# Two-layer mLSTM and band-attention trunk on one core: attention's PSUM banks, late gate transposes, rows by GpSimd's queue, modulation sums in quarters

## The chip, the cores and the metric

The kernel runs on one core of a Trainium2 chip. The metric is device time in microseconds of one execution; the time before is the median of three runs. TensorE (PE in the profile) multiplies, VectorE (DVE) and ScalarE (ACT) work element by element, GpSimd (POOL) takes a small part, and SyncE (SP) issues DMAs. PEld is PE's loading of weights. On each engine instructions run in the order in which they stand in the program; an instruction that waits holds up those behind it.

## The reference

512 tokens, model width 2048, fp32, two layers and a key/value projection between them:

```
mod  = silu(c) @ ada_w[l] + ada_b[l]             # shift, scale, gate: 3 x 2048 per layer
h    = rmsnorm(x, g_pre) * (1 + scale) + shift
layer 0: proj = h @ w_in (2048 x 16400); q, k = silu(causal_conv(...)); v, o, z; 8 mLSTM heads
         y = sigmoid(o) * rmsnorm(heads) * silu(z);  y @ w_out (4096 x 2048)
kmod = silu(c) @ kv_ada_w + kv_ada_b             # shift and scale of the shared key/value input
k, v = (rmsnorm(x, kv_g) modulated by kmod) @ kv_w
layer 1: q, z = h @ b_w_in; 16 heads: softmax(q k / sqrt(128) + relative bias, band) v
         (o * silu(z)) @ b_w_out
x    = x + gate * rmsnorm(y, g_post)             # after each layer
```

With 512 tokens and chunks of 64 with 8 chunks to the left, the band is causal by chunks over the whole sequence.

## The kernel before

Every fp32 operand of a large product is split into a rounded part and a rest (`split`, L186: a cast on ACT, a subtraction on DVE, L189), and `mm3` (L258) makes three matmuls of them. The weights of all products lie in one stream (`wst`): SP loads a raw tile (`wr`), ACT casts it to `wh`, DVE subtracts to `wl`, and in products of the Strassen kind (`proj_s`) DVE, from the keys on POOL, forms sums `ws` (L216) that are split too. PSUM is cut into five banks for projections (`newp`) and three for everything else (`newa`).

A scheduler sets the order on each engine: it follows the program, except that work under `high_priority` (weights, evacuations) is drawn forward, and instructions under `keep_in_program_order` keep their place among each other. Work that is to run beside a projection is hung on it as a hook, a function called before the weight piece of that number (`at={k: f}`).

The stages, with the start in the profiled execution: the modulation, normalised rows and the first v products (0 to 210 us); the v rows of heads 4 to 7 (`proj_b`, 210); eight mLSTM heads (411), each two `proj_s` for q and k and four for o and z, with scores, rows of v and the normaliser between; the output product `a_w_out` in four column groups, first half of the inner width, then second half, there by pairs of row tiles (1480); then residual, turning into columns (`turned`, `ps_x`, L914), values of columns 0 and 1 (1868), keys (1968), values 2 and 3 (2155), attention heads (2250), `b_w_out` (2643).

What the change and the prediction touch:

- **The modulation sums.** A column of `mod` is a dot product of `silu(c)` with 2048 weights on 128 partitions. It is done on DVE in two halves of 1024: a load of 512 KB, a multiply-and-sum, and a read of the accumulator. `background` (L602) does 64 halves (gate of layer 0, and `HALF_KV` = 16 of the 32 columns of `kmod`) beside the v rows; `late_half` (L619) does 96 more, 72 beside `a_w_out` (`first_half`) and 24 in the keys (`kv_half`); `last_gates` (L1225) does the 32 of the last gate beside `b_w_out`, and `gates_end` turns each four columns into a row (`ps_gg`, L646).
- **The gates** of the mLSTM (`gates`, L533): a long chain of 8x512 operations on DVE and ACT that ends in four small transposes into `ps_at` (L576).
- **Head sums** (`head_sums`, `head_splits`): sums of the input rows for `proj_s`, needed by the first head.
- **Rows.** `y_tile` (L843) loads the heads' results (`yr`, two buffers, 512 KB) by SP; `residual` (L879) loads the input rows `xr` by SP just before it needs them, sums squares (`sqx`) and stores; `keyed` loads `xp` by POOL's queue.
- **Attention.** `weights` (L1115) makes four score tiles `ps_s` in four tiles of three banks, then the softmax; `flipped` (L1136) transposes the weights into `ps_t`, four tiles in three banks: the tenth transpose needs the bank of the first group again, so it stands behind that group's `split`.

## Time and profile before

| | us |
|---|---|
| median of 3 runs | 2849.38 (2848.09 to 2855.21) |
| the profiled execution's own time | 2849.11 |
| its span, first to last instruction | 2847.3 |
| PE busy | 2769.4 (97%) |
| DVE busy | 2299.7 (81%) |
| ACT busy | 1507.1 (53%) |
| POOL busy | 335.5 (12%) |
| mean granted TensorE clock | 0.993 |

In the profile a group is named by its line in the kernel before, its engine, its operation and `out<-in`; an arrow in brackets with a time is the idle time of the engine before the instruction and what ended it. "Stretch" tables give the busy time of each engine between two times. The ends of matmuls are modelled, so a busy PE may still run below its pace.

### The profile page before, as it was taken

Reading aid. Unit: us, or ns where it says so; the run is one execution under the profiler, and the core shown is the slowest. Engines: PE = TensorE matmul, PEld = TensorE weight load, DVE = VectorE, ACT = ScalarE, POOL = GpSimd, SP = SyncE. Lnnn points to the kernel's source line nnn. Section 1 sums busy time; section 2 is a strip of 40 time slices with the busy share of each in tenths; the row PEclk is TensorE's granted clock in tenths of the full one; section 3 lists DMA queues with packets and bytes.
Section 4 is the critical chain, followed back from the end, with each engine's and each line's share of the span. In section 5 each row is a group of like instructions: output and inputs, shape, how many; then the busy total and the mean of one; then the engine's idle time right before and its main releaser. Section 6 shows DMA issues by size and latency. Waiting matters only on the chain.

```text
span 2847.3 us, 45749 instructions
## 1 busy us (share of the span) xinstructions
PE 2769.4 (97%) x17066; PEld 2481.5 (87%) x17066; DVE 2299.7 (81%) x4108; ACT 1507.1 (53%) x2576; POOL 335.5 (12%) x308
## 2 busy tenths in 40 slices
PE   7999999999999999999999999999999999999998
PEld 5787878999999999999998878877888899999877
DVE  7976689898989898888886676668996888888755
ACT  4222236575757575757564232477335566666523
POOL 0000000000000000000000000001660455554000
PEclk9999999999999999999999999999999999999999
DMA  8886973332323333333337886787556533333875
GB/s 325 306 301 241 300 244 110 107 123 101 127 102 123 113 115 112 112 112 112 118 109 255 298 313 231 244 290 262 204 189 212 176 120 124 131 126 124 290 256 182
DMA packets 173145, 529.39 MB, mean 186 GB/s; under 512 B 18629, under 2 KB 27365, under 8 KB 172281
## 3 DMA queue, kind: packets, MB, share of 16 engines
q1 hardware_dynamic: 172282, 524.38, 53.5%
q8 instruction: 133, 2.18, 0.3%
q0 software_dynamic: 640, 2.10, 0.2%
q14 instruction: 90, 0.74, 0.1%
HBM read 484.40 MB, written 47.24 MB: 187 GB/s over the span
## 4 chain that ended last, share of the span: by engine, by line
PE 70%; DVE 12%; DMA 11%; issue 4%; ACT 2%; SPq 0%; DVEq 0%; ACTq 0%; POOL 0%; POOLq 0%
PE ps_y L261 9%; PE ps_azo L261 8%; PE ps_bzo L261 6%; DVE wl L189 5%; PE ps_czo L261 5%; PE ps_dzo L261 5%; DMA ada<-in_adaT 4%; PE ps_azq L261 4%; DMA al<-in_adaT 4%; PE ps_kv L261 4%; PE ps_l L261 3%; PE ps_bzq L261 3%; PE ps_cz L261 2%; PE ps_czq L261 2%; PE ps_dzq L261 2%
## 5 line engine op out<-in xcount | busy, mean ns | idle before, releaser
L188 ACT CAST wh<-wr 128x384 fp32r<-128x384 f32 (+2 forms) x816 | 550.2, 674 | 939.5 <-PE ps_y L261 226.9
L189 DVE TENSOR_TENSOR wl<-wr,wh 128x384 fp32r<-128x384 f32 (+2 forms) x816 | 643.8, 789 | 259.2 <-ACT wh L188 240.7
L261 PE MATMUL ps_y<-wh,y 128*128 128x512 f32 x1536 | 479.6, 393 | 0.0
L189 DVE TENSOR_TENSOR wl<-ws,wh 128x512 fp32r<-128x512 f32 x477 | 375.8, 788 | 0.0
L261 PEld LDWEIGHTS ps_y<-wh,y 128*128 128x128 f32 x1536 | 290.5, 189 | 60.8 <-DVE z L355 0.2
L261 PE MATMUL ps_y<-wl,y 128*128 128x512 f32 x768 | 301.4, 392 | 2.6 <-DVE wl L189 2.6
L188 ACT CAST wh<-ws 128x512 fp32r<-128x512 f32 x477 | 294.1, 617 | 9.3 <-DVE ws L216 5.1
L261 PE MATMUL ps_azo<-h,wh 128*128 128x256 f32 (+1 forms) x1024 | 232.1, 311 | 0.0
L216 POOL TENSOR_TENSOR ws<-wr 128x512 f32<-128x512 f32 (+1 forms) x96 | 138.8, 1446 | 407.6 <-DVE wl L189 243.7
L216 POOL TENSOR_TENSOR ws<-ws,wr 128x256 f32<-128x256 f32 (+1 forms) x192 | 181.5, 945 | 15.0
L261 PEld LDWEIGHTS ps_y<-wl,y 128*128 128x128 f32 x768 | 145.5, 189 | 33.8 <-DVE wl L189 3.8
L261 PEld LDWEIGHTS ps_azo<-h,wh 128*128 128x128 f32 x1024 | 166.1, 191 | 8.5
L766 POOL TENSOR_TENSOR nmd<-nm,maskd 128x512 f32<-128x512 f32 x8 | 10.5, 1317 | 1365.3 <-DVE sp_q L189 922.5
L261 PE MATMUL ps_kv<-wh,hkv 128*128 128x512 f32 x512 | 160.6, 392 | 1.1 <-DVE hkv L189 0.9
L261 PE MATMUL ps_v<-wh,h 128*128 128x512 f32 x512 | 159.8, 393 | 0.0
L261 PE MATMUL ps_azo<-h,wl 128*128 128x256 f32 (+1 forms) x512 | 158.7, 310 | 0.0
L261 PE MATMUL ps_bzo<-h,wh 128*128 128x256 f32 (+1 forms) x640 | 156.7, 326 | 0.0
L261 PE MATMUL ps_czo<-h1s,wh 128*128 128x256 f32 x768 | 146.9, 283 | 0.0
L216 DVE TENSOR_TENSOR ws<-ws,wr 128x256 f32<-128x256 f32 (+1 forms) x384 | 135.0, 353 | 3.0
L261 PE MATMUL ps_l<-wh,h 128*128 128x512 f32 x384 | 120.7, 391 | 3.1 <-ACT wh L188 3.0
L261 PEld LDWEIGHTS ps_czo<-h1s,wh 128*128 128x128 f32 x768 | 120.3, 192 | 0.7
L261 PE MATMUL ps_azq<-h,wh 128*128 128x256 f32 (+1 forms) x512 | 117.1, 313 | 1.9 <-ACT wh L188 1.9
(339 smaller groups left out, 6890.0 us busy)
## 6 DMA issues: line engine op xcount, KB each, us to landing
wr<-in_wst SPq DMA_DIRECT2D x512, 512.0 KB, 3.8
ada<-in_adaT SPq DMA_DIRECT2D x160, 512.0 KB, 6.0
al<-in_adaT SPq DMA_DIRECT2D x96, 512.0 KB, 4.8
xt<-nsc SPq DMA_DIRECT2D x48, 256.0 KB, 4.6
ysc<-zo SPq DMA_DIRECT2D x32, 256.0 KB, 2.5
yr<-ysc SPq DMA_DIRECT2D x16, 512.0 KB, 5.5
vr<-vrow SPq DMA_DIRECT2D x24, 256.0 KB, 4.3
bsc<-in_ext SPq DMA_DIRECT2D x16, 320.0 KB, 6.1
```

Source lines behind the costliest of these rows:

```text
L188: cast = nc.scalar.copy(hi, src)
L189: nc.vector.tensor_tensor(lo, src, hi.bitcast(F32), op=ALU.subtract)
L216: add = lambda o, a, b: summer[0].tensor_tensor(o, a, b, op=ALU.add)
L261: nc.tensor.matmul(ps, a, b, start=start, stop=stop)
L766: nc.gpsimd.tensor_tensor(nmd, nm.rearrange("p (a b) -> p a b", a=4), maskd.unsqueeze(1).to_broadcast([P, 4, P]), op=ALU.add)
```

## The change

Five edits:

1. Attention. Scores 0 and 2 share one bank (128 + 384 columns) and are made in the order 0, 2, 1, 3; the transposes 2 and 3 share one bank (256 + 128), and all ten are issued before the first split.
2. Small gate transposes. `gates_turned` is a hook of the next head's v rows instead of the end of `gates`; `gates_end` is replaced by `last_gates(g, 0)` and, some pieces later, `gates_out`.
3. `yr` and `xr` are loaded by GpSimd's queue.
4. `xr` has buffers of its own and is loaded ahead (`residual_rows`): row tiles 0 and 1 at the start of the last column group of pair 0, 2 and 3 within the next; a copy of one column from `ssq` holds each load back to that place.
5. Modulation. Of the 32 columns of `kmod`, 8 instead of 16 go in the background (48 halves), 16 go into the heads as 64 quarters of 512 (256 KB loads), eight per head; the remaining late halves are 80, of which eight stand beside pair 0 of `a_w_out`, and none in the keys. The hooks of `turned(1)` move by two pieces.

```
-HALF_KV = 16
+HALF_KV = 8
+QUARTERS = 16
@@ gates
         nc.sync.dma_start(gsc[1], w)
+
+    def gates_turned():
         pt = newa("ps_at")
         for j in range(4):
-            nc.tensor.transpose(pt[:, j * 8 : j * 8 + 8], e[:, j * P : (j + 1) * P], ident[:8, :8])
+            nc.tensor.transpose(pt[:, j * 8 : j * 8 + 8], ssum[:8, j * P : (j + 1) * P], ident[:8, :8])
@@ late sums
+    heads_end = 96 + HALF_KV + QUARTERS
+    late_cols = [*range(heads_end, 128)], [*range(48, 64)], [*range(64, 80)]
+    quarters = [(j, i) for j in range(4) for i in range(96 + HALF_KV, heads_end)]
+    def late_part(parts, w, sc, tile=None):
         for j, i, t in begun:
             tc.keep_in_program_order(nc.vector.tensor_tensor_reduce(
...
+        j, i = parts.pop(0)
+        if sch[0] != (j, w):
+            sch[:] = (j, w), sc([P, w], F32, tag="sc", name=f"sch{w}_{i}_{j}")
+            nc.sync.dma_start(sch[1], scd[j * w : (j + 1) * w].partition_broadcast(P))
+        t = tile([P, w], F32, tag="al", name=f"al{w}_{j}_{i}")
+        tc.keep_in_program_order(nc.sync.dma_start(t, adaT[i, :, j * w : (j + 1) * w]))
+    def late_half(tile=None):
+        late_part(halves, D // 2, scp.tile, tile)
@@ v rows
         if h == FIRST:
             add_at(at, {8: gates})
+        if h == FIRST + 1:
+            add_at(at, {2: gates_turned})
@@ heads
+    def quarter():
+        late_part(quarters, S, lp1.tile, lp2.tile)
+    lp1, lp2 = hst.enter_context(pool("lsc")), hst.enter_context(pool("lal", bufs=2))
-            zs = pair((i // 2) * (V0 // 2) + h * DK, f"zq{h}_{i}")
+            zs = pair((i // 2) * (V0 // 2) + h * DK, f"zq{h}_{i}", {4: quarter})
         for i in range(4):
+            add_at(hooks[i], {k: quarter for k in ((4,), (3, 6), (2,), (2, 5))[i]})
@@ y_tile
-                nc.sync.dma_start(raw, ysc[h, :, q : q + 2, :])
+                nc.gpsimd.dma_start(raw, ysc[h, :, q : q + 2, :])
@@ residual
+    def residual_rows(m):
+        p, tag = (tp, "f") if m % 2 == 0 else (np_, "xr")
+        xrs[m] = [p.tile([P, 2 * S], F32, tag=tag, name=f"xr{m}_{i}", bufs=2) for i in range(2)]
+        for i in range(2):
+            nc.vector.tensor_copy(xrs[m][i][:, 0:1], ssq[:, 4 * m + 2 : 4 * m + 3])
+            nc.gpsimd.dma_start(xrs[m][i], xN[m, :, 2 * i * S : 2 * (i + 1) * S])
...
-            xr = tp.tile([P, 2 * S], F32, tag="f", name=f"xr{m}_{i}", bufs=2)
-            nc.sync.dma_start(xr, xN[m, :, d])
@@ a_w_out, second half
+        elif pair == 0:
+            if g == 3:
+                residual_rows(0)
+                residual_rows(1)
+            at = {k: y_half for k in range(2, KT, 4)}
...
+            add_at(at, {k: lambda m=m: residual_rows(m) for k, m in ((2, 2), (6, 3))})
@@ keys
-        add_at(at, {k: kv_half for k in (0, 2, 4)})
@@ weights
+        both = newa(f"ps_s{h}_0")
+        for i in (0, 2, 1, 3):
+            n = P * (i + 1)
+            ps = both[:, :P] if i == 0 else both[:, P:] if i == 2 else newa(f"ps_s{h}_{i}")[:, :n]
@@ flipped
+        pts, pss = [], [newa(f"ps_t{h}_{j}") for j in range(3)]
+        pss = [pss[0], pss[1], pss[2], pss[2][:, 256:]]
+        for j in range(4):
+            for i in range(j, 4):
+                nc.tensor.transpose(pss[j][:, P * (i - j) : P * (i - j + 1)], pr[i][:, P * j : P * (j + 1)], ident)
@@ last gates
-                add_at(hooks, {8: lambda g=g: gates_end(g)})
+                add_at(hooks, {8: lambda g=g: last_gates(g, 0), 12: lambda g=g: gates_out(1, 4 * g, 4 * g + 4)})
...
+                add_at(hooks, {2: lambda: last_gates(2, 0)} | {k: lambda: last_gates(3, 2) for k in range(4, 12, 2)})
+                add_at(hooks, {6: lambda: gates_out(1, 8, 12)})
+                add_at(hooks, {12: lambda: last_gates(3, 0), 14: lambda: gates_out(1, 12, 16)})
```

Where the instructions come to stand is settled by the scheduler. Three places follow; the line numbers are each kernel's own (the changed kernel's are one higher up to about L570, then more), and a number at the end of a name is a tile's.

PE in the v rows, around the four transposes of the gates (`ps_at`; the matmuls `ps_v` beside it are those of heads 4 and 5). Before:

```order
L261 MATMUL ps_v_0_1720<-wl_0_2063,h_14_1334 128x512
L261 MATMUL ps_v_0_1720<-wh_0_2062,h_14_1334 128x512
L261 MATMUL ps_v_0_1720<-wh_0_2062,h_15_1472 128x512
L261 MATMUL ps_v_0_1720<-wl_0_2063,h_15_1472 128x512
L576 MATMUL ps_at<-kcs,ssum 128x8 x4
L261 MATMUL ps_v_0_1720<-wh_0_2062,h_15_1472 128x512
L261 MATMUL ps_v_1_1721<-wh_0_2062,h_14_1334 128x512
```

and now:

```order
L262 MATMUL ps_v_2_2098<-wl_0_2111,h_1_310 128x512
L262 MATMUL ps_v_2_2098<-wh_0_2110,h_1_310 128x512
L262 MATMUL ps_v_3_2099<-wh_0_2110,h_1_310 128x512
L262 MATMUL ps_v_3_2099<-wl_0_2111,h_1_310 128x512
L262 MATMUL ps_v_3_2099<-wh_0_2110,h_1_310 128x512
L579 MATMUL ps_at<-kcs,ssum 128x8 x4
L262 MATMUL ps_v_0_2096<-wh_0_2153,h_2_384 128x512
L262 MATMUL ps_v_0_2096<-wl_0_2154,h_2_384 128x512
```

The transposes stood among the last matmuls of head 4's group; they now stand 43 matmuls further on, between two weight pieces of head 5's.

DVE at the end of the v rows (ISA rows with `ada` are the background's multiply-and-sum, `h1r` and `h1s` the head sums, `wl` the weights' splits, `ws` the sums of the first head's weights). Before:

```order
L189 TENSOR_TENSOR wl_0_3030<-wr_3027,wh_0_3029 128x1024
L216 TENSOR_TENSOR ws_3127<-ws_3127,wr_3125 128x128
L420 ISA ada_0_2741,mod<-ada_0_2741,scB,cl 128x1024
L420 ISA mod 128x1
L216 TENSOR_TENSOR ws_3127<-ws_3127,wr_3125 128x128
L420 ISA ada_1_2746,mod<-ada_1_2746,scB,mod 128x1024
L420 ISA mod 128x1
L661 TENSOR_TENSOR h1r_0_2794<-h_0_274 128x512
L661 TENSOR_TENSOR h1r_1_2795<-h_1_310 128x512
L189 TENSOR_TENSOR wl_0_3067<-wr_3064,wh_0_3066 128x1024
```

and now:

```order
L421 ISA ada_0_2502,mod<-ada_0_2502,scB,cl 128x1024
L421 ISA mod 128x1
L190 TENSOR_TENSOR wl_0_2662<-wr_2659,wh_0_2661 128x1024
L421 ISA ada_1_2504,mod<-ada_1_2504,scB,mod 128x1024
L421 ISA mod 128x1
L669 TENSOR_TENSOR h1r_0_2746<-h_0_274 128x512
L669 TENSOR_TENSOR h1r_1_2747<-h_1_310 128x512
L671 TENSOR_TENSOR h1r_0_2746<-h1r_0_2746 128x256
L669 TENSOR_TENSOR h1r_0_2791<-h_2_384 128x512
L672 TENSOR_TENSOR h1r_0_2746<-h1r_0_2746,h1r_1_2747 128x256
L669 TENSOR_TENSOR h1r_1_2792<-h_3_420 128x512
L190 TENSOR_TENSOR wl_0_2719<-wr_2716,wh_0_2718 128x1024
```

Before, the head sums begin behind the last `ada`, when the `ws` of the first head already stand beside them; now the last `ada` comes eight weight splits before the stage's end, and the head sums stand among those splits.

DVE in the second head, around the reciprocal of the normaliser of the first (`dd`). Before:

```order
L216 TENSOR_TENSOR ws_6464<-ws_6464,wr_6462 128x2x128
L216 TENSOR_TENSOR ws_6524<-wr_6522 128x256
L816 TENSOR_SCALAR dd_6248<-dd_6248 128x512
L216 TENSOR_TENSOR ws_6524<-ws_6524,wr_6522 128x128
L189 TENSOR_TENSOR wl_0_6469<-wr_6462,wh_0_6468 128x384
L216 TENSOR_TENSOR ws_6524<-ws_6524,wr_6522 128x128
L189 TENSOR_TENSOR wl_0_6469<-ws_6464,wh_0_6468 128x512
L818 RECIPROCAL dd_6248<-dd_6248 128x512
L189 TENSOR_TENSOR wl_1_6496<-wr_6462,wh_1_6495 128x384
L189 TENSOR_TENSOR wl_1_6496<-ws_6464,wh_1_6495 128x512
```

and now:

```order
L217 TENSOR_TENSOR ws_6536<-wr_6534 128x256
L831 TENSOR_SCALAR dd_6255<-dd_6255 128x512
L217 TENSOR_TENSOR ws_6536<-ws_6536,wr_6534 128x128
L626 ISA al_0_119_6144,mod<-al_0_119_6144,sch_104_0_3191,cl 128x512
L626 ISA mod 128x1
L190 TENSOR_TENSOR wl_0_6481<-wr_6474,wh_0_6480 128x384
L190 TENSOR_TENSOR wl_0_6481<-ws_6476,wh_0_6480 128x512
L217 TENSOR_TENSOR ws_6536<-ws_6536,wr_6534 128x128
L833 RECIPROCAL dd_6255<-dd_6255 128x512
L190 TENSOR_TENSOR wl_1_6508<-wr_6474,wh_1_6507 128x384
L190 TENSOR_TENSOR wl_1_6508<-ws_6476,wh_1_6507 128x512
```

A quarter (`al`, with its accumulator's read) now stands ahead of a weight split and of the reciprocal.

More of the change, by code (lines that the diff above doesn't have):

```diff
@@ L624, in late_half @@
         begun.clear()
[L625 removed]
+        if not parts or tile is None:
             return
[L627 to L632 removed]
+        j, i = parts.pop(0)
[4 more added lines that the diff above has]
+        tc.keep_in_program_order(nc.sync.dma_start(t, adaT[i, :, j * w : (j + 1) * w]))
         begun.append((j, i, t))
+    def late_half(tile=None):
+        late_part(halves, D // 2, scp.tile, tile)
     def add_at(at, more):
@@ L826, in amul_cols @@
         )
+    quarter()
+    assert not quarters
     hst.close()
@@ L969, in hybrid_trunk @@
             at = {k: first_half for k in range(0, KT, 2)}
+        elif pair == 0:
[3 more added lines that the diff above has]
+            at = {k: y_half for k in range(2, KT, 4)}
         elif pair == 1 and g == 2:
-            late_half()
+            y_half()
+            assert not halves, len(halves)
+            amul_cols(2 * KT, 48 + KT, GPRE + KT)
             amul_cols(KT, 96 + KT, KVG)
@@ L1030, in hybrid_trunk @@
         for g in range(2):
-            turn = {4 * i: lambda i=i: turned(1, [i], True) for i in range(4)} if pair == 0 and g == 1 else {}
+            turn = {2 + 4 * i: lambda i=i: turned(1, [i], True) for i in range(4)} if pair == 0 and g == 1 else {}
             if pair:
@@ L1042, in hybrid_trunk @@
     zp = zst.enter_context(pool("zp", bufs=2, side="right"))
-    alp = zst.enter_context(pool("late", bufs=1, side="right"))
     for i in range(KT // 2):
@@ L1052, in hybrid_trunk @@
     kst.close()
-    late_half()
-    assert not halves, len(halves)
-    amul_cols(2 * KT, 48 + KT, GPRE + KT)
     ast = ExitStack()
@@ L1136, in flipped @@
     def flipped(h, pr):
-        pts = []
+        pts, pss = [], [newa(f"ps_t{h}_{j}") for j in range(3)]
[3 more added lines that the diff above has]
+                nc.tensor.transpose(pss[j][:, P * (i - j) : P * (i - j + 1)], pr[i][:, P * j : P * (j + 1)], ident)
         for j in range(4):
             n = S - P * j
-            ps = newa(f"ps_t{h}_{j}")
-            for i in range(j, 4):
-                nc.tensor.transpose(ps[:, P * (i - j) : P * (i - j + 1)], pr[i][:, P * j : P * (j + 1)], ident)
+            ps = pss[j]
             if j < 3:
```

39 lines of the change are left out of this document (12 added, 27 removed).

## The prediction

> **What bounds the kernel now.** I read part 1 of the page first: which engine is full.
>
> ```profile
> span 2847.3 us, 45749 instructions
> PE 2769.4 (97%) x17066; PEld 2481.5 (87%) x17066; DVE 2299.7 (81%) x4108; ACT 1507.1 (53%) x2576; POOL 335.5 (12%) x308
> ```
>
> TensorE (PE) is idle for 2847.3 - 2769.4 = 77.9 us. The change neither adds nor removes matrix work, so it can win only what PE loses by waiting, and lose what it makes PE wait for. The profiled execution took 2849.11 us, 1.8 more than its span and 0.3 less than the median of the three runs, 2849.38; the sum is made against 2849.1.
>
> Second, the table of stretches, to see where PE loses. Columns: stretch, length, busy time (count) of PE, PEld, DVE, ACT, POOL, then granted PE clock, DMA share, GB/s.
>
> ```profile
> 264.00:284.00 20.00, 14.98 (x59) 11.94 (x58) 12.78 (x17) 7.54 (x10) 0.00 (x0) 0.83 0.41 143
> 400.00:446.00 46.00, 40.77 (x228) 34.04 (x228) 45.34 (x104) 20.96 (x43) 1.46 (x1) 0.96 0.36 121
> 446.00:1480.00 1034.00, 1034.00 (x7413) 980.27 (x7412) 917.68 (x1852) 675.57 (x1133) 9.08 (x7) 1.00 0.33 113
> 1500.00:1525.00 25.00, 22.91 (x105) 19.03 (x105) 19.89 (x31) 17.15 (x28) 0.00 (x0) 0.93 0.70 242
> 1525.00:1840.00 315.00, 312.43 (x1376) 257.67 (x1375) 208.74 (x272) 102.89 (x139) 0.00 (x0) 1.00 0.77 269
> 1840.00:1965.00 125.00, 117.45 (x537) 93.34 (x536) 88.63 (x134) 95.56 (x177) 5.60 (x10) 1.00 0.88 300
> 1965.00:2155.00 190.00, 175.39 (x1334) 166.94 (x1333) 171.35 (x244) 81.24 (x154) 103.74 (x95) 0.98 0.57 198
> 2250.00:2640.00 390.00, 384.81 (x3049) 374.79 (x3048) 330.78 (x698) 262.85 (x544) 202.37 (x183) 1.00 0.39 129
> 2664.00:2680.00 16.00, 13.33 (x61) 10.87 (x60) 12.93 (x20) 6.62 (x12) 0.00 (x0) 0.89 0.88 309
> 2718.00:2740.00 22.00, 16.78 (x68) 13.46 (x67) 12.41 (x18) 3.22 (x4) 0.00 (x0) 0.84 0.72 254
> ```
>
> I count a stretch's loss as its idle time plus (1 - clock) x busy, because after a long stall PE is granted less clock: 264-284 loses 5.0 + 0.17 x 15.0 = 7.6. In the same way 400-446 loses 6.9, the mLSTM heads (446-1480) nothing, 1500-1525 3.7, 1525-1840 2.6, the residual and turning part (1840-1965) 7.6, the keys (1965-2155) 14.6 + 3.5 = 18.1, attention 5.2, 2664-2680 4.1, 2718-2740 7.9. Third, the waits, which name what PE waits for (total, times, longest):
>
> ```profile
> PE ps_ck L261 <- DVE zk L352: 6.7, 6, 1.7
> PE ps_gg L646 <- DVE ggate L644: 5.5, 2, 5.2
> PE ps_at L576 <- DVE ssum L567: 5.0, 1, 5.0
> PE ps_x L914 <- ACT sqx L886: 5.0, 3, 2.6
> PE ps_t L1142 <- DVE pt L189: 4.7, 11, 2.7
> ...
> PE ps_q L261 <- ACT sp_q L188: 2.1, 1, 2.1
> ```
>
> Each of the six lies at a place that the change edits. They are single late results, not a full engine, so moving the consumer or the producer can remove them.
>
> **The change part by part.**
>
> *Gate transposes later: -7 us.* `ps_at` waits 5.0 us for `ssum`, the end of a chain on VectorE and ScalarE. In the order it now stands 43 matmuls of 512 columns further on. Their pace, and what a stall does to it, stand in the timeline around the `ps_gg` stall:
>
> ```profile
> 2718.53 0.61 PE L261 MATMUL ps_y<-wh,y 128*128 128x512 f32 x2
> ...
> 2719.21 0.61 PE L261 MATMUL ps_y<-wh,y 128*128 128x512 f32 x2
> ...
> 2731.16 0.37 PE L646 MATMUL ps_gg<-kcs,ggate 128*4 128x128 f32 x1 [5.22 <-DVE ggate L644]
> ...
> 2731.76 1.06 PE L261 MATMUL ps_y<-wh,y 128*128 128x512 f32 x2
> ...
> 2733.04 1.06 PE L261 MATMUL ps_y<-wh,y 128*128 128x512 f32 x2
> ```
>
> Three matmuls start every 0.68 us (0.227 each), after the stall every 1.28. 43 x 0.227 = 9.8 us, more than the 5.0 missing. Next to be late would be `aT`, which nobody reads before the heads. Between 0 and -7.6; I take -7.
>
> *Entry into the heads: -6.* VectorE is busy 45.34 of 46 us here; its last background reduction runs up to 401.7, and the head sums follow it:
>
> ```profile
> 400.45 1.28 DVE L420 CUSTOM_DVE_ANT_0 ada<-ada,scB,mod 128x1024 f32<-128x1024 f32 x1
> ```
>
> 16 of the 64 halves, some 16 x 1.36 = 22 us of VectorE with their accumulator reads, leave this background. In the order the head sums now stand before the stage's end, among the weight splits of the last v projection. PE then finds the sums ready, and only the weights of the first head are left to wait for. Of 6.9 I take 6 (3 to 6.9).
>
> *Quarters in the heads: +3.* 64 reductions of 128x512. The nearest row with that shape and form:
>
> ```profile
> L1129 DVE CUSTOM_DVE_ANT_0 s<-ps_s,bias x64: 275/481/693, 2273.8 to 2656.1; 128x128 f32<-128x128 f32 x16, 128x256 f32<-128x256 f32 x16, 128x384 f32<-128x384 f32 x16, 128x512 f32<-128x512 f32 x16
> L1129 DVE DVE_READ_ACCUMULATOR2_ANT mx<- x64: 75/79/84, 2274.0 to 2656.7; 128x1 f32 x64
> ```
>
> 0.69 + 0.08 = 0.77 us each, 8 per head: 6.2 us. One head takes 135.8 us (the same matmul groups come back at that distance), and VectorE is busy 917.68 / 1034 = 89%, so on the average there are 15 us of room. But the room is uneven:
>
> ```profile
> 573.00:607.00 34.00, 34.00 (x242) 31.99 (x241) 33.90 (x70) 21.06 (x37) 0.00 (x0) 1.00 0.41 140
> ```
>
> For 34 us after the reciprocal VectorE is full, and one quarter is put right ahead of that reciprocal:
>
> ```profile
> 567.72 0.69 DVE L189 TENSOR_TENSOR wl<-ws,wh 128x512 fp32r<-128x512 f32 x1
> 569.46 3.35 DVE L818 RECIPROCAL dd<-dd 128x512 f32<-128x512 f32 x1 [1.04 <-ACT dd L817]
> ```
>
> There VectorE idles 1.04 us, which covers this quarter (0.77). With that cover gone, the weight splits behind the reciprocal come 0.77 us later, and PE takes the first of them next. Of the other seven, up to two fall into the full stretch. The ends are 0 and 8 x 2.6 x 0.77 = 16; I take 3, half a quarter per head, nearer to the covered case. The DMAs that come with them, 64 of 256 KB, find a DMA share of 0.33.
>
> *Rows by GpSimd's queue: -1.* In 1500-1525 PE waits 2.1 us for `sp_q`, whose cast stands on ScalarE behind casts of `y` that wait for `yr`. SP spends 9.72 us on four `yr` issues, with the weights behind them:
>
> ```profile
> 1503.75 9.72 SPq L849 DMA_DIRECT2D yr<-ysc  x4
> 1514.90 0.33 SPq L208 DMA_DIRECT2D wr<-in_wst  x1
> ```
>
> The weights no longer queue there, but the casts of `y` keep their place on ScalarE ahead of `sp_q`, so I take only -1 of the 3.7 (+4 to -3.7). What GpSimd's queue costs is seen in its eight loads of `xp`, half as large, in 1850-1960:
>
> ```profile
> xt<-nsc SPq DMA_DIRECT2D x10, 256.0 KB, 5.5
> ...
> xp<-nsc POOLq DMA_DIRECT2D x8, 256.0 KB, 5.0
> ```
>
> They land no later than SP's loads of the same size. The Trainium skill, "SBUF — State Buffer", section "SBUF: two separate sides", speaks against this part: a load issued by GpSimd has its descriptors written in software through a port that VectorE can hold, so the load waits for VectorE, and the page advises the queue of SP or ScalarE. The eight rows show no such delay, so the sum stands; by the rule it would be the second rival's.
>
> *Residual rows ahead: -4.* PE waits 5.0 us in three waits for `sqx`; ahead of it VectorE waited for `xr`:
>
> ```profile
> 1847.41 1.28 DVE L884 SCALAR_TENSOR_TENSOR y<-y,rsn,xr 128x1024 f32<-128x1024 f32 x1 [1.96 <-DMA xr<-in_xN]
> ```
>
> Now the eight loads precede, each pinned by a 128x1 copy on VectorE (under 0.1 us) that waits for a column of `ssq`, with weight splits queued behind it; GpSimd issues them between `yr` and `xp`. But pair 0's transposes also stand some 11 us earlier in PE's order, which spends part of the slack. Of 7.6 I take 4 (+4 to -7.6).
>
> *Keys: -12.* 24 late halves leave, 23 of them in this stretch:
>
> ```profile
> L621 DVE CUSTOM_DVE_ANT_0 al<-al,sch,mod 128x1024 f32<-128x1024 f32 x15 | 21.0, 1400 | 8.2 <-DMA al<-in_adaT 8.1
> L621 DVE CUSTOM_DVE_ANT_0 al<-al,sch,cl 128x1024 f32<-128x1024 f32 x8 | 12.4, 1548 | 3.1 <-DMA al<-in_adaT 3.1
> ```
>
> 33.4 us of VectorE's 171.35; it falls to 73%. What PE waits for is the release of `ps_ck` by L352, a short operation that queues on VectorE behind such a 1.4 us piece (longest wait 1.7). The weight splits stay in that queue. Of 18.1 I take 12 (5 to 18.1).
>
> *Rows stage, 1525-1840: +1.* Eight of the halves (8 x 1.36 = 11 us; VectorE is at 66%) come here, with changes of the condition's half between them. The price of such a change is seen once, VectorE idle for 7.10 us, and the stretch as a whole loses 2.6:
>
> ```profile
> 1637.34 1.29 DVE L621 CUSTOM_DVE_ANT_0 al<-al,sch,cl 128x1024 f32<-128x1024 f32 x1 [7.10 <-DMA al<-in_adaT]
> ```
>
> I take +1 (0 to 5.2, the same loss twice more).
>
> *Attention -5, its last head -3.5.* The tenth transpose of a head stands alone behind the splits that free its bank: ten waits, 4.7 - 2.67 = 2.1 us; for the last head, with less work between, one of 2.67 us, and the clock falls to 0.89:
>
> ```profile
> 2670.25 0.47 PE L1142 MATMUL ps_t<-kcs,s 128*128 128x128 f32 x1 [2.67 <-DVE pt L189]
> ```
>
> Now all ten stand together in three banks, and the scores need three instead of four. What is late next is the first split of `ps_t`, which `ps_o` reads a head later. I take 5 of 5.2 (1 to 8: ends of matmuls are modelled and hide short gaps) and 3.5 of 4.1 (0 to 4.1).
>
> *Last gates: -5.* `ps_gg` stands 26 matmuls (5.9 us) later against a stall of 5.2. But its input is paced by loads, and PE comes 4.1 us earlier if the last head's stall goes; then 5.2 - 5.9 + 4.1 = 3.4 us stay and the clock falls again. Between -7.9 and -2.5; I take -5, about the middle.
>
> Sum: -7 - 6 + 3 - 1 - 4 - 12 + 1 - 5 - 3.5 - 5 = -39.5, so 2849.1 - 39.5 = **2809.6 us**, told as 2809.
>
> **The rivals.**
>
> *Heads partly bound by VectorE.* All of the 16 instead of 3: 2823. For it: 33.90 of 34 us. Against it: the other 100 us of a head have the room.
>
> *GpSimd's loads are slow.* A pair of `y` tiles feeds 24 matmuls, 5.45 us; two buffers give a cycle of 10.9. A landing of 5 to 6 and some 2 us of casts and splits fit; a landing of 10, twice the row's 5.0, does not: some 2 us short on each reuse, three reuses of each buffer in the first group, and again in the second half: +12, so 2822. For it: 512 KB, double that row. Against it: no late landing seen. It is also what the skill's rule would give.
>
> *Gains half given back.* Stretches with DMA shares of 0.70 to 0.88 (1500-1965, 2664-2740) keep the pace of their loads, and the keys their chain of releases: half of the 43.5 us of gains, 2831.
>
> *Slower: the quarters are on the path.* Place: the heads, all eight quarters, each ahead of a weight split that PE waits for. 64 x 0.77 = 49 us, so 2849.1 - 42.5 + 49 = 2856; with one stall per head long enough for the half pace seen after 2731 (2 us), 2872. It decides from (42.5 + 8.5) / 8 = 6.4 us a head. Against it: VectorE's 15 us of room.
>
> *The change does not do what it says.* The stalls come back at the new places, on the same late results, and only the keys gain: some 6 us, 2843.
>
> **How the numbers follow.** Forecast (2795 to 2820): 0.49. Heads partly bound 0.13, GpSimd's loads 0.10, half given back 0.15, slower 0.07, not what it says 0.06. A tie is within 0.3%, 8.5 us, about what a measurement here can tell. Faster: 0.49 + 0.13 + 0.10 + 0.15 = 0.87, less 0.01 for a deeper case of the loads, 0.86; same 0.06; slower 0.08. The low end, 2790, is where keys and attention reach their far ends (6 + 3), the heads cost nothing (3) and the gates and the residual rows go whole (3 + 4); the high end, 2838, is past the half case.
>
> **What would show it.** Right: `ps_at` and the lone `ps_t` gone from PE's waits; `ps_ck` under 2 us; PE full in the heads with VectorE near 94%; `ps_gg` at or below 3.4 us. Wrong: PE waiting for `wl` in the heads and a clock below 1.00 there; ScalarE waiting longer for `yr`; `ps_x` still behind `sqx`; PE's loss in the keys above 13 us.

## The result, and the profile after

The changed kernel takes **2827.7 us** (median of 4 runs, 2824.0 to 2831.2) against 2851.6 before (4 runs); the ratio of the runs is 0.9916, 95% interval 0.9896 to 0.9936. It is faster by 0.8%, 24 us by the medians, where 2809, 40 us less, was forecast. The time lies inside the range (2790 to 2838) and outside the forecast's own band (2795 to 2820). The two profiled executions stand at 2831.2 and 2849.1, so the traces show 18 us of it; all times by stage below are from them. One execution of one experiment (e_gates_in_values, the last below), its profiled one, took 9451.9 us with a granted clock of 1.00, which nothing here explains, and it is left out of that kernel's time.

The first part of the page of the changed kernel:

```profile
span 2829.0 us, 45873 instructions
PE 2761.8 (98%) x17066; PEld 2478.6 (88%) x17066; DVE 2294.5 (81%) x4180; ACT 1480.0 (52%) x2557; POOL 336.0 (12%) x332
```

PE has the same 17066 matmuls and is idle for 67.2 us instead of 77.9. Only 10.7 us of the gain is idle time; the rest is PE running closer to its pace (the clock, and the short gaps behind modelled ends).

The table of stretches of the changed kernel, cut at the stages' new places (columns as before: length; PE, PEld, DVE, ACT, POOL; clock; DMA share; GB/s):

```profile
260.00:292.00 32.00, 29.16 (x123) 23.44 (x122) 23.27 (x28) 9.72 (x12) 0.00 (x0) 0.95 0.64 203
400.00:446.00 46.00, 46.00 (x300) 42.19 (x299) 31.14 (x62) 20.77 (x38) 1.29 (x1) 1.00 0.43 141
562.00:1478.00 916.00, 909.89 (x6479) 857.65 (x6479) 832.35 (x1729) 566.65 (x969) 7.78 (x6) 1.00 0.39 129
...
1529.00:1855.00 326.00, 315.08 (x1368) 256.96 (x1367) 220.45 (x298) 104.46 (x148) 5.78 (x11) 0.99 0.79 277
1855.00:1985.00 130.00, 123.74 (x569) 100.33 (x568) 97.77 (x155) 102.86 (x187) 10.98 (x19) 1.00 0.86 297
1985.00:2155.00 170.00, 168.68 (x1341) 165.07 (x1340) 123.38 (x189) 75.54 (x146) 95.42 (x90) 1.00 0.41 144
2240.00:2630.00 390.00, 389.74 (x3115) 383.18 (x3115) 350.81 (x706) 267.03 (x555) 196.99 (x183) 1.00 0.40 134
2640.00:2690.00 50.00, 49.51 (x226) 40.79 (x226) 32.80 (x54) 17.80 (x31) 0.00 (x0) 1.00 0.88 311
2690.00:2740.00 50.00, 44.79 (x186) 36.39 (x185) 31.02 (x44) 11.14 (x17) 0.00 (x0) 0.93 0.73 257
```

The entry into the heads (400 to 446), the keys (1985 to 2155) and attention are now nearly full: PE idles 0.0, 1.3 and 0.3 us there. Three stretches are worse than their counterparts of before: the heads, which had lost nothing, are 6.1 us short; the output product (1529 to 1855) is 10.9 short where it had been 2.6; and in 2690 to 2740 there still is a stall of 5.2.

The waits of the changed kernel say what those are:

```profile
PE ps_y L262 <- DVE wl L190: 7.7, 9, 1.6
PE ps_y L262 <- ACT sqy L884: 5.7, 2, 5.2
...
PE ps_y L262 <- ACT y L964: 4.6, 1, 4.6
...
PE ps_v L262 <- ACT vk L503: 4.0, 2, 2.8
...
PE ps_dzo L262 <- ACT wh L189: 3.9, 7, 0.8
...
PE ps_q L262 <- ACT sp_q L189: 2.5, 1, 2.5
```

Of the six waits that the prediction quoted, `ps_ck`, `ps_gg`, `ps_at`, `ps_t` and `ps_x` for `sqx` have left the top of the list. But `ps_v`, `ps_y` for `sqy`, `ps_y` for the copy `y` and `ps_dzo` are new, and all four are waits for ScalarE. The longest entry, for the weight splits `wl` of the output product, is a wait for VectorE; it was 2.6 us before.

To see where the 18 us come from, I take the distance between the first matmuls of named groups (for the end, the last `ps_o` and the last `ps_y`), which the traces give for every kernel:

| stage, from first to first | before | changed | difference | forecast |
|---|---|---|---|---|
| start (to `ps_v`) | 218.4 | 220.1 | +1.7 | 0 |
| v rows (`ps_v` to `ps_azq`) | 191.6 | 190.5 | -1.1 | -7 |
| entry (`ps_azq` to the first head's `ps_q`) | 149.8 | 140.2 | -9.6 | -6 |
| heads (to `ps_y`) | 944.0 | 956.6 | +12.6 | +3 |
| output product and turning (`ps_y` to `ps_kv`) | 364.3 | 379.7 | +15.4 | -4 with the next row |
| values 0 and 1 (to `ps_ak`) | 99.0 | 94.2 | -4.8 | |
| keys, values 2 and 3 (to `ps_dz`) | 273.9 | 252.5 | -21.4 | -12 |
| attention with its last head (to the last `ps_o`) | 435.9 | 423.1 | -12.8 | -8.5 |
| last product (to the last `ps_y`) | 160.4 | 161.9 | +1.5 | -5 |

The rows add up to -18.5 us; behind the last `ps_y` the changed kernel takes 0.2 us longer, so the spans differ by 18.3. Three of the forecast's gains came, each half as large again or more; 28 us of them were given back in two stages, and the two gains of the gates did not come.

Each time by stage is that of one execution. How far it can be trusted is seen where several kernels have the same program in a stage, the changed kernel and those of the first experiments below: entry, heads, keys and attention agree within 2 us between their traces, but the v rows stand anywhere from 190.5 to 195.6 us, the output product with GpSimd's rows from 373.2 to 379.7, values 0 and 1 from 94.2 to 97.4, and the last product from 159.3 to 163.7. Differences of a few us in these four stages can be chance.

### The profile page after: what moved, and what is told of

Same layout as the page of the kernel before. It is cut to its first block, busy times and chain, and to the rows that moved or that the text cites. A ratio compares the mean times of both kernels' runs of the same rounds, so it can differ in the third digit from the quotient of the medians.

```text
span 2829.0 us, 45873 instructions
## 1 busy us (share of the span) xinstructions
PE 2761.8 (98%) x17066; PEld 2478.6 (88%) x17066; DVE 2294.5 (81%) x4180; ACT 1480.0 (52%) x2557; POOL 336.0 (12%) x332
## 4 chain that ended last, share of the span: by engine, by line
PE 73%; issue 10%; DMA 8%; DVE 6%; ACT 3%; POOL 0%; SPq 0%; DVEq 0%; ACTq 0%; POOLq 0%
PE ps_y L262 8%; PE ps_azo L262 6%; PE ps_bzo L262 4%; PE ps_kv L262 4%; PE ps_czo L262 4%; PE ps_dzo L262 4%; PE ps_azq L262 4%; PE ps_l L262 3%; PE ps_az L262 3%; PE ps_cz L262 3%; PE ps_dz L262 3%; PE ps_v L262 3%; DMA ada<-in_adaT 3%; PE ps_bzq L262 3%; PE ps_dzq L262 2%
## 5 line engine op out<-in xcount | busy, mean ns | idle before, releaser
L190 DVE TENSOR_TENSOR wl<-ws,wh 128x512 fp32r<-128x512 f32 x477 | 359.0, 753 | 0.2 <-ACT wh L189 0.2
L217 POOL TENSOR_TENSOR ws<-wr 128x512 f32<-128x512 f32 (+1 forms) x96 | 129.4, 1348 | 399.8 <-DVE wl L190 168.3
L262 PEld LDWEIGHTS ps_v<-wh,h 128*128 128x128 f32 x512 | 97.0, 189 | 25.3 <-ACT vk L503 4.8
```

The source lines that it names most:

```text
L190: nc.vector.tensor_tensor(lo, src, hi.bitcast(F32), op=ALU.subtract)
L217: add = lambda o, a, b: summer[0].tensor_tensor(o, a, b, op=ALU.add)
L262: nc.tensor.matmul(ps, a, b, start=start, stop=stop)
```

## The experiments

Two theories stood against each other after the result. **Order on ScalarE and travel of late results**: an operand that comes late holds the next instruction on an in-order engine, so moving its reader only passes the stall to what stands behind. **Resources**: VectorE is too full in the heads, GpSimd's queue and the DMA too slow in the output product. In the first set each kernel undoes or moves one thing in the changed kernel; in the second each adds one part of the change to the kernel before. The before times are those of the same chips, 2849.6 to 2851.3 for all of them.

### The heads' hooks moved

```
-            add_at(hooks[i], {k: quarter for k in ((4,), (3, 6), (2,), (2, 5))[i]})
+            add_at(hooks[i], {k: quarter for k in ((2, 5), (3, 6), (), (2, 5))[i]})
```

> The changed kernel with the eight quarters of a head at other pieces (o/z pair 0: 2 and 5, pair 2: none), so VectorE does the same work per head. In the changed kernel PE loses about 1.9 us in each of heads 1 to 7 at one place, where ScalarE does a sigmoid and a silu with their two table loads back to back (3.8 us) ahead of the next weight cast; with these hooks four weight casts stand between them again. Theory (order on ScalarE): the place closes, 7 x 1.9 = 13 us, so 2815 against the changed kernel's 2828. Rival (VectorE is too full for the quarters): the loss stays or moves within the head, 2828 within 4.

The place is at 637 to 642 us of the changed kernel. ScalarE's timeline there, and below it the same place of the kernel before:

```profile
638.10 1.28 ACT L803 ACT_TABLE_LOAD   x1
639.39 0.63 ACT L803 ACTIVATE zo<-zo 128x512 f32<-128x512 f32 x1
640.04 1.28 ACT L804 ACT_TABLE_LOAD   x1
641.33 0.63 ACT L804 ACTIVATE zo<-zo 128x512 f32<-128x512 f32 x1
641.87 0.49 ACT L189 CAST wh<-wr 128x384 fp32r<-128x384 f32 x1
```

```profile
645.45 1.28 ACT L788 ACT_TABLE_LOAD   x1
646.74 0.64 ACT L788 ACTIVATE zo<-zo 128x512 f32<-128x512 f32 x1
647.28 0.50 ACT L188 CAST wh<-wr 128x384 fp32r<-128x384 f32 x1
...
649.25 1.28 ACT L789 ACT_TABLE_LOAD   x1
650.55 0.63 ACT L789 ACTIVATE zo<-zo 128x512 f32<-128x512 f32 x1
```

Before, four weight casts stand between the sigmoid (L788) and the silu (L789). In the changed kernel the pair (L803, L804) stands in one block with its two table loads, 3.8 us long, and the first weight cast behind it comes at 641.87; PE's next product needs it and stands 0.75 us, then again for the split. This is so in heads 1 to 7 and not in head 0. The block alone costs nothing: the fourth o/z pair of a head stands in one block in the kernel before too, and PE has no wait in those heads. It costs where weight casts that PE needs next stand behind it.

With the hooks moved, the eight quarters of a head cost the same on VectorE, and the casts are back between the two. The kernel took 2822.9 us (4 runs, 2816.2 to 2826.2; ratio to before 0.9902, 0.9887 to 0.9917). That interval overlaps the changed kernel's; the stage's time is clearer. The heads went from 956.6 to 948.5 us, and the traces agree: five with the changed kernel's hooks have 954.7 to 956.6, three with the moved ones (this kernel and two below) 948.5 to 949.3. The table of the heads' stretch in this kernel:

```profile
562.00:1478.00 916.00, 915.22 (x6540) 865.22 (x6540) 841.87 (x1741) 571.71 (x977) 7.78 (x6) 1.00 0.39 129
```

VectorE is busier than in the changed kernel (841.87 for 832.35, 92%) and PE idles 0.8 us instead of 6.1; no wait for `wh` or `wl` is left in the heads. So the order on ScalarE carries the 8.1 us that the moved hooks won back of the 12.6, and VectorE's load is not the cause of these. The other 4.5 us, about 0.6 a head, are VectorE's. PE's loading of weights shows them, in a wait that the heads of the kernel before do not have:

```profile
PEld ps_s L262 <- DVE qk L190: 2.7, 7, 0.6
```

The weights of the score matmuls `ps_s` come from the split of `qk` on VectorE, which is 92% busy. Laid matmul by matmul beside the kernel before, this kernel falls behind by 0.4 to 0.9 us in each of seven heads, nearly all of it at `ps_s`. The changed kernel falls behind by 0.3 us there and by 1.2 to 1.6 at the block. So the quarters do cost VectorE's time at one place of each head; which part of it the new order of `qk` adds is not separated.

### The rows back on SP

```
-                nc.gpsimd.dma_start(raw, ysc[h, :, q : q + 2, :])
+                nc.sync.dma_start(raw, ysc[h, :, q : q + 2, :])
```

> The changed kernel with the y rows (yr) loaded by SP's queue again, the residual rows still by GpSimd's. In the changed kernel PE loses some 22 us in 1500 to 1850 against 9 before, at weight splits and at the copies of the accumulators, which stand on ScalarE behind casts that wait up to 12.5 us for yr. Theory (GpSimd's queue brings yr late): the loss goes back to about 10, so 2816. Rival (the 80 late halves with two more reloads of the condition's half crowd SP's queue and the DMA): nothing changes, 2828 within 3, or worse, since SP takes the 16 loads back.

The output product's largest stall in the changed kernel, from ScalarE's timeline:

```profile
1697.97 0.62 ACT L189 CAST y<-yr 128x512 fp32r<-128x512 f32 x1 [5.51 <-DMA yr<-ysc]
...
1699.96 1.55 ACT L964 COPY y<-ps_y 128x512 f32<-128x512 f32 x3
```

The copies of the accumulators (L964) stand behind a cast that waits 5.5 us for `yr`. PE cannot begin the next column group until they have freed its banks: that is the 4.6 us in the list of waits. How long such a load takes stands in the listing of the tile `yr`, of the changed kernel first, and then with SP's queue:

```profile
L866 POOL DMA_DIRECT2D yr<-ysc x16: 527/527/681, 1494.1 to 1694.1; - x16
...
DMA to landing us min/median/max: 3.8/5.2/9.2
```

```profile
L866 SPq DMA_DIRECT2D yr<-ysc x16: 319/326/422, 1496.7 to 1684.5; - x16
...
DMA to landing us min/median/max: 4.4/5.5/6.2
```

The medians agree; by GpSimd's queue the longest took 9.2 us. By SP the output product took 367.7 us instead of 379.7, and the kernel 2824.4 (4 runs, 2821.5 to 2826.1; 0.9912, 0.9895 to 0.9929). The stage's gain of 12 us in the traces is not found again in the medians, 3 us apart, whose ranges overlap. Four traces with GpSimd's `yr` and the new modulation (the changed kernel, e_heads and the two gate kernels below) have 379.7, 377.8, 373.2 and 378.9, four with SP's 367.7, 369.1, 372.9 and 371.9: means 377.4 and 370.4. The queue costs about 7 us there, not 12; the direction is shown, the size only roughly. Another 6 us stay with SP's queue: three traces with the output product of before (before, and the attention and the gate part alone, below) have 362.1 to 365.7.

Both kinds of row back on SP:

```
-                nc.gpsimd.dma_start(raw, ysc[h, :, q : q + 2, :])
+                nc.sync.dma_start(raw, ysc[h, :, q : q + 2, :])
-            nc.gpsimd.dma_start(xrs[m][i], xN[m, :, 2 * i * S : 2 * (i + 1) * S])
+            nc.sync.dma_start(xrs[m][i], xN[m, :, 2 * i * S : 2 * (i + 1) * S])
```

> The changed kernel with both yr and the residual rows (xr) loaded by SP's queue, xr still ahead of its use. If GpSimd's queue is slow for 512 KB loads (xr landed in 6.5 to 12.6 us there, 5.4 before), PE's loss in 1850 to 1887 of 5 us falls by 2 to 4 beyond the kernel with yr alone on SP: about 2813. Rival (the DMA rings are simply full there, 0.90 to 0.95): no difference from that kernel.

2822.9 us (4 runs, 2818.3 to 2826.3; 0.9904, 0.9889 to 0.9919): no difference from `yr` alone on SP. The residual rows landed late by GpSimd's queue (median 9.3 us in the changed kernel), but they are loaded so early that nobody waits long for them. The expected 2 to 4 us did not come.

### The gate row by another queue

```
-        nc.sync.dma_start(ggd[layer, a:b], row)
+        (nc.gpsimd if layer else nc.sync).dma_start(ggd[layer, a:b], row)
-        nc.sync.dma_start(gb, ggd[layer, 4 * g : 4 * g + 4, :]...
+        (nc.gpsimd if layer else nc.sync).dma_start(gb, ggd[layer, 4 * g : 4 * g + 4, :]...
```

> The changed kernel with the second layer's gate row (store of the turned gates, and its load spread over the partitions) by GpSimd's queue. In the changed kernel PE stands 5.2 us at 2725, since the evacuation of the first column group waits for the gate row: the store waited 3.6 us and the load 6.4 us on SP behind loads of modulation weights that wait for buffers. Theory (SP's queue holds the gate row up): the stall and the half pace behind it go, 8 us, so 2820. Rival (the gates themselves are paced by their loads, as forecast): at most 2 us.

The stall that replaced `ps_gg`, in the changed kernel, by SP, by VectorE and by PE:

```profile
2717.48 0.28 SPq L657 DMA_DIRECT2D ggd<-gg  x1
...
2724.15 0.38 SPq L880 DMA_DIRECT2D ssum<-ggd  x1
```

```profile
2729.19 2.48 DVE L883 TENSOR_TENSOR yo<-ps_y,ssum 128x512 f32<-128x512 f32 x4
```

```profile
2730.66 0.80 PE L262 MATMUL ps_y<-wh,y 128*128 128x512 f32 x1 [5.21 <-ACT sqy L884]
```

ScalarE has copied the turned gates to SBUF at 2713.9 (2713.60 and 0.25), but the store is issued at 2717.48 and the load at 2724.15, and the accumulators are scaled from 2729.19 (when the row landed before that is not recorded), which frees their banks. In the kernel before, SP did the same for this row without such waits, in some 6 us from the copy at 2731.8, since the load landed 4.0 to 4.5 us after its issue:

```profile
2731.85 0.27 SPq L649 DMA_DIRECT2D ggd<-gg  x1
...
2733.51 0.33 SPq L863 DMA_DIRECT2D ssum<-ggd  x1
```

With GpSimd's queue the kernel took 2831.8 us (4 runs, 2830.6 to 2835.6), 4 more than the changed kernel, so the expected 8 us did not come. The wait on SP's queue is gone in its trace: the copy ends at 2719.1 and the store goes at 2719.38. But the transfers took longer: the load went at 2723.85, behind the store's landing, and the row was there at 2731.1, 7.3 us later. The stall at this place is 3.0 us instead of 5.2, while the first column group, which had waited 0.5, waits 4.3 for its row, whose load took 6.6. SP's queue does hold the row up in the changed kernel, but the other queue gives the time back. What turns this into a stall is that the turning now stands 6 us later on PE: there are only 13.0 us (2712.45 to 2725.45, 56 matmuls) from there to the first matmul that needs one of the banks.

### Parts of the change alone

The attention part alone on the kernel before (its edit is the change's, in `weights` and `flipped`):

```
+        for i in (0, 2, 1, 3):
+            ps = both[:, :P] if i == 0 else both[:, P:] if i == 2 else newa(f"ps_s{h}_{i}")[:, :n]
...
+        pss = [pss[0], pss[1], pss[2], pss[2][:, 256:]]
```

> The kernel before with the attention part alone. In the changed kernel the stretch from the first z product to the last head's output lasts 423.1 us against 435.9 before. Theory (the lone tenth transpose and the fourth score bank cost this by themselves): 423 to 425 again, so 2851 - 12 = 2839. Rival (part of it came from VectorE and the loads being less crowded): 430, 2845.

2838.6 us (7 runs; 0.9956, 0.9936 to 0.9976), attention 424.4 us. The part stands by itself and gives what it gave in the whole.

The later gate transposes alone:

```
+        if h == FIRST + 1:
+            add_at(at, {2: gates_turned})
...
+                add_at(hooks, {8: lambda g=g: last_gates(g, 0), 12: lambda g=g: gates_out(1, 4 * g, 4 * g + 4)})
```

> The kernel before with the later gate transposes alone (both layers). Theory (a late result is found by the next instruction in order: the copies of head 4's accumulators behind the gates' last exponential on ScalarE, 2.8 us, and the gate row on its way through memory, 5.2 us): the stalls stay with another name, v rows and last product together 2 us shorter at most, 2849. Rival (the prediction: the stalls go): 12 us shorter, 2839.

2848.3 us (10 runs; 0.9992, 0.9980 to 1.0004): nothing that can be told from zero. The v rows take 192.0 us and the last product 162.0. The first of the two stalls that came instead is to be seen on ScalarE in the changed kernel:

```profile
271.21 1.28 ACT L573 ACT_TABLE_LOAD   x1
277.02 0.63 ACT L573 ACTIVATE gate_w<-gate_w 8x512 f32<-8x512 f32 x1 [4.53 <-DVE gate_w L572]
277.56 1.03 ACT L503 COPY vk<-ps_v 128x512 f32<-128x512 f32 x2
```

The same chain of gates that had made `ps_at` late makes the last exponential late, and two copies of head 4's accumulators stand behind it; PE waits for their banks 2.8 us (`ps_v` for `vk`; 3.3 in the trace of this part alone), with the clock at 0.95 around it. In the last product it is the gate row, as above: PE waits 6.0 us for `sqy` in the trace of this part, where it had waited 5.5 for `ps_gg`.

The modulation part alone:

```
+HALF_KV = 8
+QUARTERS = 16
...
-        add_at(at, {k: kv_half for k in (0, 2, 4)})
```

> The kernel before with the modulation part alone (8 columns from the background and 16 columns of late halves into the heads as quarters, none left in the keys; rows still by SP). The sigmoid and silu of the second o/z pair stand back to back on ScalarE here too. Theory: entry into the heads -9.6, heads +12 (order on ScalarE), keys and values after them -20, output product within +4 of before's 364.3: about 2836. Rival (the late halves' new places make the output product slow, not GpSimd's queue): output product 375 or more, about 2847.

2850.5 us (10 runs; 0.9998, 0.9984 to 1.0013), near neither of the two expectations. By itself this part is worth nothing that can be told from zero: entry -9.9, heads +12.2, keys with values 2 and 3 -12.1, and smaller differences (output product +3.2, v rows +3.1, attention and the last product +1.4 each), none of which stands clear of what traces of equal stages differ by. Its gain goes into the heads, where the sigmoid and the silu stand in one block here too. And the keys gain only 12 of the 21 us that they gain in the whole change.

The rows part alone:

```
+                nc.gpsimd.dma_start(raw, ysc[h, :, q : q + 2, :])
...
+                residual_rows(0)
+                residual_rows(1)
```

> The kernel before with rows by GpSimd's queue and residual rows ahead, alone. Theory (GpSimd's queue brings yr late, ScalarE's casts wait for it with the accumulators' copies behind them): output product 364.3 + 8 or more, values after it -3: 2855. Rival (the prediction: a gain of 5 from rows that lie ready): 2846.

2846.4 us (10 runs; 0.9985, 0.9970 to 1.0000), against 2855 and 2846 expected: the prediction's side. Output product +2.9, values 0 and 1 -1.6, keys -6.3 us. The output product's +2.9 is hardly outside the 362.1 to 365.7 above, so GpSimd's queue costs some 3 us or less with the old modulation, and some 7 with the new one. The gain in the keys is new to both theories, but it is not the keys' own: the waits for `ps_ck` stay (7.0 us in six waits, before 6.7). Laid matmul by matmul beside the kernel before, 6.7 us are won in the first 240 of the stage's 1701 matmuls (1967 to 2010 before), right behind residual and turning. It is the gain of that part on the other side of the border between the stages; whether the rows ahead or the moved `turned` hooks brought it, no run separates.

The four parts sum to 11.4 + 1.8 - 0.5 + 3.6 = 16.3 us by their medians, the whole to 24. The 95% intervals of the five are 3 to 6 us either way, so these times alone do not show that the parts depend on each other. By stages they do in one place: in the output product +3.2 and +2.9 alone became +15.4 together in the one trace, about +13 in the mean of four. In the keys -12.1 and -6.3 make up most of the -21.4.

### The gates' sources earlier

```
-            add_at(at, {8: gates})
+            add_at(at, {4: gates})
...
+                add_at(hooks, {k: lambda g=g: last_gates(2 * g, 2) for k in range(0, 8, 2)})
+                add_at(hooks, {k: lambda g=g: last_gates(2 * g + 1, 2) for k in range(8, 16, 2)})
```

> The changed kernel with both gates' sources earlier instead of only their readers later: the mLSTM gates start two weight pieces earlier (hook 4 for 8), so that their last exponential stands on ScalarE ahead of the copies of head 4's accumulators with its input ready; the last gates' sums run on without a pause from the first piece of the last product, so that the second column group's gates are done before that group begins and its row has the whole group to travel. Theory (a late source finds the next reader): both stalls go, 2.8 + 5.2 us and the half pace behind them, about 10: 2818. Rival (the loads of the sums cannot run faster, DMA share 0.88 there): the last product gains nothing or loses, 2826.

2842.4 us (9 runs; 0.9969, 0.9959 to 0.9978): 15 us slower than the changed kernel. The rival held, and more than it said. In the v rows the 2.8 us went and the stretch remained at 191.1, because a second wait for copies `vk`, those of head 6's accumulators, stands there in its place:

```profile
363.95 0.79 PE L262 MATMUL ps_v<-wh,h 128*128 128x512 f32 x1 [3.67 <-ACT vk L503]
```

This one comes with the new modulation. The head sums now stand among the last weight splits, and their casts (`h1s`), which wait for VectorE, stand on ScalarE between the copies. The changed kernel waits 1.1 us there, the modulation part alone 1.9, other kernels with it up to 4.1, and the kernels with the old modulation nothing. So what the entry into the heads won is paid back in part one stage earlier.

The last product took 175.8 us, with these waits:

```profile
PE ps_y L262 <- ACT y L189: 6.9, 1, 6.9
PE ps_gg L654 <- DVE ggate L652: 6.4, 3, 2.8
PE ps_y L262 <- DVE wl L190: 2.6, 1, 2.6
```

and ScalarE's timeline at the first of them:

```profile
2686.36 1.14 ACT L189 CAST y<-y2r 128x512 fp32r<-128x512 f32 x2 [11.93 <-DMA y2r<-y2c]
```

The sums run on without a pause, their loads stand on SP waiting for buffers, and the product's own input (`y2r`) comes 11.9 us late behind them. SP's queue, with the DMA at 0.86 to 0.88 in 2625 to 2700, has no place for earlier sums there.

### Versions for both troubles

Heads' hooks and SP's `yr` together (the two edits above):

> The changed kernel with the heads' hooks moved and yr by SP, both undone troubles together. If the two are independent: 5 + 3 to 8 below the changed kernel's 2828, so 2815 to 2820, with heads at 948 and output product at 368.

**2817.6 us** (4 runs, 2814.6 to 2823.6; 0.9888, 0.9872 to 0.9903), in the expected range: 34 us under the kernel before and 10 under the changed kernel, whose runs (from 2824.0) all lie above these. Heads 949.3, about as expected, output product 372.9, where 368 was expected.

With both gates' sources earlier as well:

> The changed kernel with the heads' hooks moved, yr by SP and both gates' sources earlier. If the three are independent, 10 below the kernel with the first two: 2806 to 2810, faster than both kernels. If the last product's loads hold it: 2815.

2830.2 us (5 runs; 0.9929, 0.9915 to 0.9942), last product 175.2: the same loss of some 13 us as above, and neither of the two expectations.

Last, the heads' hooks and SP's `yr`, with the first four of the last 16 gate columns moved to the values, so that the sums of the others run a column group ahead:

```
-    late_cols = [*range(heads_end, 128)], [*range(48, 64)], [*range(64, 80)]
+    late_cols = [*range(heads_end, 128)], [*range(48, 64)], [*range(64, 80)], [*range(80, 84)]
...
+        values(g, range(4), at | {k: lambda: late_half(alp.tile) for k in (0, 4, 8, 12)})
...
+                add_at(hooks, {k: lambda g=g: last_gates(g + 1, 2) for k in (4, 6, 8, 10)})
```

> The changed kernel with the heads' hooks moved, yr by SP, and the first four of the last 16 gate columns (eight halves) summed beside values 2 and 3, where PE loses nothing and the DMA share is 0.58. The last product's other 24 halves then run one column group ahead, so every gate row has a whole group to travel, with no more loads at the product's start than in the changed kernel. Theory (rows late because sources are late, and the product's start has no DMA left for earlier sources): last product 160 to 155 or less, no wait for the gate row, total 2817 - 8 = 2809. Rival (the moved halves cost beside the values what they save later, VectorE there at 84%): 2817 again.

2817.9 us (4 runs, 2814.2 to 2820.4; 0.9885, 0.9868 to 0.9901): the same as without it, on the rival's side. There is no trace of these four, so where the 8 us went stays open.

## Why the prediction was right and where it was not

The direction, three of the places of the gains and the range held. That the time fell inside the range is partly luck: by stages the terms missed by 38 us in one direction and by 17 in the other. By its own terms:

- **Entry into the heads**, -6 forecast, -9.6 measured: right, the whole of the stretch's loss went. The term came out short by caution and by counting 6.9 lost where start-to-start it was 9.9.
- **Keys**, -12 forecast, -21.4: the mechanism was right (`ps_ck` has left the waits; VectorE 123.38 of 170 us, 73% as forecast), the size too small. The part alone gives 12.1, just the term. Of the other 9, 6.3 come with the rows part by itself: they belong to the term of the residual rows, whose gain the prediction had looked for in front of the keys.
- **Attention and its last head**, -8.5 forecast, -12.8 (-11.5 by the part alone): right in place and cause. The loss was read from busy time, whose modelled ends hide short gaps; the prediction gave that as its upper bound.
- **Gate transposes in the v rows**, -7 forecast, -1.1: wrong. "Next to be late would be `aT`, which nobody reads before the heads" was the step that failed. It followed the value that `ps_at` makes; it did not follow the chain's other end, the exponential of `gate_w`, which stands on ScalarE among the copies that free PSUM banks (2.8 us of waiting for 5.0). A second wait of the same kind, 1.1 us and more, came from the head sums of the entry's term.
- **Last gates**, -5 forecast, +1.5: wrong in the same way. The +1.5 itself is within what traces differ by; what failed is the gain. The step reckoned what was left of the `ps_gg` stall and not the row's way from there, store and load, which took up to 15.3 us in the changed kernel; `ps_gg` moved 5.9 us later used up what that way had to spare, and the stall came back with the same 5.2 us for `sqy`.
- **Quarters in the heads**, +3 forecast, +12.6: the rival "heads partly bound by VectorE" came out in size (16 at most), but only a third of it in cause. Two thirds, 8.1 us, is the block of sigmoid and silu on ScalarE that the new hooks led the scheduler to, and it went with other hooks while VectorE had the same work. The 4.5 us that stay are VectorE's, near the 3 forecast, but at the split of `qk` in front of the scores and not at the reciprocal. The prediction looked at the order of VectorE alone for this term.
- **Rows by GpSimd's queue, rows stage and residual rows**, -4 together, +10.6 measured (+15.4 and -4.8): the rival "GpSimd's loads are slow" (+12) came true in part. The prediction took eight small loads of 5.0 us as evidence, and quoted the Trainium skill, "SBUF — State Buffer", section "SBUF: two separate sides", against it. With 512 KB the median stayed at 5.2 us, but the longest were 9.2 and, for the residual rows, 12.6. For `yr` the long ones go with the queue: 8.8 by GpSimd with the old modulation too, 6.2 at most by SP with the new one. The residual rows land late by SP's queue as well, with a median of 7.6 us (5.6 before, 9.3 by GpSimd), so there the queue is only a part of it. Whether the cause in GpSimd's queue is the one that the page names, descriptors held up by VectorE, no run here shows. The queue's share is about 7 of the 15.4. The term that was missing is the same as in the other three: ScalarE's casts wait in order, with the accumulators' copies behind them. The residual rows themselves gained what was forecast or more, in the keys; their pinning copies took 0.14 us each, not under 0.1.

The three gains that came, 9.6 + 21.4 + 12.8 = 43.8 us, are as large as all that were forecast (43.5). What they were reduced by was, for the most part, results that came late to an engine that works in order, and only for some 5 us VectorE's load. The rival "half given back" gave the nearest time (2831) by a wrong cause.

## What to carry to other kernels

When a stalled reader is moved later, list everything else that waits for the same late result, on every engine, and what stands behind each of those in order; a stall is gone only if nothing on that list frees a buffer or a PSUM bank that the busy engine needs. When hooks are moved under a scheduler, read the new order of all engines around each hook, above all of the one with the long blocks (here ScalarE's table loads), and not only of the engine that gets the work. Parts of a change that share an engine are worth timing apart: here one of four carried half of the gain, two carried nothing, and a small shift of hooks and one queue put back were worth another 10 us.

## What the runs showed of the hardware that was not expected

A sigmoid and a silu of 128x512 on ScalarE take 0.63 us each, but 3.8 us in a block, since each brings a table load of 1.28 us.

A gate row of 2 KB that is stored and loaded back spread over 128 partitions was under way for some 6 us in the kernel before, by SP; for up to 15.3 us in the changed kernel (2713.9 to 2729.2), where SP issued the store 3.6 us late and the load 6.4 us after the store; and for 12 us (2719.1 to 2731.1) by GpSimd's queue with nothing in front of it.
